# Low parts of attention values at byte 132 instead of 130, and two figures of the planner

## The chip, the cores and the metric

One NeuronCore of a Trainium2 chip runs the kernel. The metric is the device time of one launch in microseconds (us). Three runs of the kernel before took 1343.99, 1344.91 and 1344.94 us; their median is 1344.91.

The engines work side by side, each through its own list of instructions: TensorE (PE in the profile; PEld is its weight load), VectorE (DVE), ScalarE (ACT), GpSimd (POOL), and SyncE (SP), which here mainly issues DMA transfers. They wait for each other by semaphores.

## The reference

Two layers of a diffusion backbone over 1024 latent tokens and 256 context tokens of width 1024, in float32. Cut to what matters:

```python
for i in range(2):
    mod_x = (silu_c @ w_mod[i] + b_mod[i])[:, None, :]      # shift, scale and gate for the tokens
    mod_c = silu_cc @ w_mod[i] + b_mod[i]                   # the same for the context
    hx = rms_norm(x, norm_g[i]) * (1.0 + sc_x) + sh_x
    hc = rms_norm(ctx, norm_g[i]) * (1.0 + sc_c) + sh_c
    # layer A (i = 0): 16 query heads on 4 key/value heads, rotary positions, softmax over 1280 keys
    # layer B (i = 1): 16 heads, 8 x 16 neighbourhood on a 64 x 16 grid with a bias, plus 256 context keys
    #   o = softmax(q k^T / 8 [+ bias]) v ;  yx = (o * silu(z)) @ w_out
    x = x + g_x * yx
return rms_norm(x, final_norm_g)
```

The attention output is, for each query and head, a weighted sum of the value rows v (64 numbers per head). That sum is the place of the change.

## The kernel before

**Two halves for each number.** Matmul operands are float16. To keep float32 accuracy each operand is kept as a high part (the number rounded to float16) and a low part (the rest, rounded again), and a product is three matmuls: high x high, high x low, low x high.

**The value tiles.** Layer A keeps the values of all 1280 keys in `v1` (line 767): 128 partitions, 10 key blocks, 4 heads, and a row of 130 float16 numbers, 260 bytes. Numbers 0 to 63 of a row are the high part, 64 is a constant (so that the same matmul also sums the weights), and from 65 on comes the low part, 64 numbers from byte 130. One number is unused. Layer B has the same row in `v1_` (line 1490), for two heads at a time. ScalarE writes the high part and VectorE the low part by a subtraction (lines 891 and 892 in `kv_post`, lines 1546 and 1547 in `put_v`).

**Who reads them.** The softmax weights of a block of 128 queries are the stationary operand, the value row is the moving one, and the result is accumulated in PSUM.

- Layer A, `pv_mm` (lines 1136 to 1138), called by `a_att`: for each key block and each of four query blocks three matmuls, weights high x value high with the constant (65 columns), weights high x value low (64 columns, from byte 130), weights low x value high (65 columns).
- Layer A, `q_att` (lines 1211 and 1213), for a quarter of the heads' work, in which scores have the queries on the partitions and the weights are turned by a DMA transpose: one matmul with 128 columns, the high part and the low part as two runs of 64, and one of weights low x value high with 64 columns.
- Layer B, `b_att` (lines 1646, 1648, 1649): the same three as in `pv_mm`.

**Stages.** The start normalises the tokens and computes the modulation of layer A and its keys and values (0 to about 100 us). Then come eight head pairs of layer A, with the projections of the next pair mixed in (to about 700 us), layer A's output projection and the normalisation for layer B (to about 810 us), eight head pairs of layer B with projections mixed in (to about 1310 us), and the output projection with the last norm.

**Modulation matmuls.** They multiply float32 weights by two vectors only, so they use 32 of the 128 columns of the array each, four side by side. `quarters` (line 600) and `cols` (line 609, 2 columns of output) serve the start; `mod_block` (lines 633 and 637) computes the other shifts, scales and gates in 16 half blocks of 16 (every second one of 20) matmuls, spread over layer A's attention. The profile shows each of these float32 matmuls as two rows.

**What sets the order.** The program is first written in the order of the Python code, with a timeline that mixes the generators. Then the class `Planner` orders the instructions of each engine anew. `cost` gives each instruction a duration; `schedule` plays the program through with these, five engines side by side; `deadlines` works backwards from that to a due time for each instruction, in which TensorE's own start times count without their idle parts; `refine` repeats this five times and keeps the order whose planned end comes first; `apply` fixes it. The planner runs before the program is built, so its figures change the order of instructions and nothing else. For TensorE `cost` takes

```python
return max(cols * passes / 2.4 + 2.5, 29.0), 170.0
```

with `passes` 4 for float32, and `schedule` lets a matmul in a 32-column strip hold the engine for 7 ns if the strip differs from that of the matmul ahead (a quarter of its cost if it is the same).

Of the kernel before, what the change touches and what calls it, by code (L numbers as in the profile page):

```python
# [13 lines left out]
F16 = mybir.dt.float16  # L14
# [7 lines left out]
P = 128  # L22
# [6 lines left out]
HD = 64  # L29
# [13 lines left out]
class Planner:  # L43
# [72 lines left out]
    def cost(self, x, rd, wr):  # L116
# [6 lines left out]
        if e == "PE":  # L123
            f32 = ins[0].dtype == mybir.dt.float32
            cols = self.elems(outs[0])
            passes = (2 if x.is_transpose else 4) if f32 else 1
            if f32 and any("idf" in a.bass_ap.tensor.name for a in ins):
                passes = 2
            return max(cols * passes / 2.4 + 2.5, 29.0), 170.0
        if k == "InstDmaTransposeAnt":  # L130
# [159 lines left out]
    def schedule(self, key=None, margin=0.0, scale=None):  # L290
# [65 lines left out]
        while count < N:  # L356
# [43 lines left out]
            if e == "PE":  # L400
# [4 lines left out]
                if ts[1] < 128 and pe_last and pe_last[0] == ts and pe_last[1] != tp:  # L405
                    t[e] = max(s + 7, t[e])
                    pe_hold = max(pe_last[2], s + occ)
                    t[e] = s + 7
                    pe_last = (ts, tp, pe_hold)
                else:  # L410
                    if pe_last and pe_last[0] == ts and ts[1] < 128:
                        pass
                    t[e] = s + (occ if ts[1] == 128 else occ / 4)
                    pe_last = (ts, tp, s + occ)
# [41 lines left out]
    def deadlines(self, margin):  # L456
# [4 lines left out]
        for a in self.order["PE"]:  # L461
            idle += max(0.0, start[a] - prev)
            prev = max(prev, start[a] + (cst[a][0] if tuple(self.node[a].tile_size or (128, 128))[1] == 128
                                         else cst[a][0] / 4))
            due[a] = start[a] - idle
# [58 lines left out]
def trunk_kernel(ctx, tc, x, cx, cc, norm_g, ng_row, b_cols, sel_c, w_m0, w_mb, b_mod, a_wkv, a_wq, a_qg, a_kg, a_w_out,  # L524
# [241 lines left out]
    k2 = ap.tile([P, NKV, TOK], F16, name="k2")  # L766
    v1 = ap.tile([P, NT, NKV, 130], F16, name="v1")
    G.memset(k2[64:65], 1.0)
# [120 lines left out]
    def kv_post(ps, t):  # L889
        vv = ps[:, 256:512].rearrange("p (h d) -> p h d", d=HD)  # L890
        S.copy(v1[:, t, :, 0:HD], vv)
        V.tensor_tensor(v1[:, t, :, 65:129], vv, v1[:, t, :, 0:HD], op=ALU.subtract)
        k16 = norm_rope_split(lp, sqk, ps[:, 0:256].rearrange("p (h d) -> p h d", d=HD), None, 1, NKV, t, gck, gsk, gks,
# [238 lines left out]
    def pv_mm(pv, hi, lo, v, n, first, last):  # L1132

        for t in range(n):
            c = slice(t * P, (t + 1) * P)
            T.matmul(pv[:, t, :], hi[:, c], v[:, 0:65], start=first and t == 0, stop=False)  # L1136
            T.matmul(pv[:, t, 0:HD], hi[:, c], v[:, 65:129], start=False, stop=False)  # L1137
            T.matmul(pv[:, t, :], lo[:, c], v[:, 0:65], start=False, stop=last and t == n - 1)  # L1138
# [32 lines left out]
    def q_att(u, pt_):  # L1171
# [7 lines left out]
        for t in range(4):  # L1179
# [17 lines left out]
            for c, (k0, n) in enumerate(KCH):  # L1197
# [9 lines left out]
                def pvs(ppt=ppt, k=k, k0=k0, t=t):  # L1207
                    for x_ in range(k):
                        kt = k0 // P + x_
                        vv = v1[:, kt, g, :].rearrange("p (a b) -> p a b", b=65)[:, :, 0:HD]  # L1210
                        T.matmul(pv[:, t, :].rearrange("p (a b) -> p a b", b=HD), ppt[:, x_], vv,  # L1211
# [273 lines left out]
    def b_qk(u):  # L1485
# [3 lines left out]
        q2 = q2z[u % 2]  # L1489
        v1_ = bq.tile([P, NT, 2, 130], F16, name=f"bv1{u}", tag="v1")  # L1490
        G.memset(v1_[:, :, :, HD:HD + 1], 2.0 * WS * WS)
# [47 lines left out]
    def b_vz(u):  # L1539
# [3 lines left out]
        def put_v(src, ts):  # L1543
            n = len(range(NT)[ts])
            vv = src[:, 0:n * P].rearrange("p (t h d) -> p t h d", h=2, d=HD)
            S.copy(v1_[:, ts, :, 0:HD], vv)
            V.tensor_tensor(v1_[:, ts, :, 65:129], vv, v1_[:, ts, :, 0:HD], op=ALU.subtract)

# [37 lines left out]
    def b_att(u):  # L1586
# [14 lines left out]
        for hf in range(2):  # L1601
            og = bl.tile([P, 4, P], F32, name=f"bog{u}{hf}", tag="og", bufs=2)
            for i in range(2):
                tq = tabs[2 * u + i]
                pv = psum.tile([P, 4, P], F32, name=f"bpv{u}{i}{hf}", tag="pv", bufs=2)
                for t0 in (hf * 4, hf * 4 + 2):
# [21 lines left out]
                    for t in (t0, t0 + 1):  # L1628
# [15 lines left out]
                        def pvs(pv=pv, pht=pht, plt=plt, i=i, t=t, keys=list(near[t]) + [NX, NX + 1]):  # L1644
                            for x_, kt in enumerate(keys):
                                T.matmul(pv[:, t % 4, 0:65], pht[:, x_], v1_[:, kt, i, 0:65],
                                         start=t % 4 == 0 and x_ == 0, stop=False)
                                T.matmul(pv[:, t % 4, 0:HD], pht[:, x_], v1_[:, kt, i, 65:129], start=False, stop=False)
                                T.matmul(pv[:, t % 4, 0:65], plt[:, x_], v1_[:, kt, i, 0:65], start=False,
# [195 lines left out]
```

## Time and profile before

| | |
|---|---|
| runs | 1343.99, 1344.91, 1344.94 us |
| profiled execution | 1345.52 us, of which 1343.7 from the first to the last instruction |
| TensorE busy | 1309.6 us (97%) |
| VectorE, ScalarE, GpSimd busy | 1067.1, 969.0, 891.2 us |
| mean granted clock of TensorE | 0.992 of full speed |
| DMA | 191.64 MB, 143 GB/s on average |

Durations of matmuls overlap: a matmul starts while the ones before it are still on their way through the array. What one costs in a row of matmuls is the distance from its start to the next start, and the duration also holds its way through. "L1137" is line 1137 of the kernel. A row of a group gives the engine, the operation, output and inputs by their names in the program, the shape, the count, and busy time with the mean duration, or shortest, median and longest.

### The profile page before, as it was taken

What the parts mean: (1) busy time and instruction counts of PE and PEld (TensorE: products, weight loads), DVE (VectorE), ACT (ScalarE), POOL (GpSimd) and SP (SyncE); (2) the same over time, 40 slices, a digit from 0 to 9 for tenths busy, and PEclk for the clock granted to TensorE, in tenths of its full rate; (3) what the DMA queues carried; (4) which work ended last, traced back from release to release, by engine and by line L of the source; (5) the groups of instructions that cost most, each with busy time, mean ns of one, the idle gap of its engine ahead of it and who ended that gap; (6) DMA issues with size and microseconds to landing.
All of it is one profiled execution on the core that took longest, in us unless ns stands there. A gap on an engine that the chain in (4) does not pass through costs nothing.

```text
span 1343.7 us, 38645 instructions
## 1 busy us (share of the span) xinstructions
PE 1309.6 (97%) x15100; PEld 928.6 (69%) x15100; DVE 1067.1 (79%) x2456; ACT 969.0 (72%) x2076; POOL 891.2 (66%) x1214
## 2 busy tenths in 40 slices
PE   8999999999999999999999989999999999999996
PEld 4457777777777777776654457869687786968552
DVE  5898787888889787769528997878888888887665
ACT  4554889988888777798743456878878888887453
POOL 2323878777777767687876467677676868767543
PEclk9899999999999999999999999999999999999998
DMA  9633576786675222244317962678777877669952
GB/s 371 188 116 96 111 152 117 145 187 135 140 145 122 74 67 72 59 119 108 113 51 187 243 139 82 125 145 152 150 139 142 158 143 162 145 151 226 286 130 110
DMA packets 390496, 191.64 MB, mean 143 GB/s; under 512 B 349792, under 2 KB 355104, under 8 KB 390312
## 3 DMA queue, kind: packets, MB, share of 16 engines
q1 hardware_dynamic: 389736, 189.13, 62.1%
q8 instruction: 118, 1.93, 0.6%
q14 instruction: 66, 0.54, 0.1%
q10 hardware_dynamic: 576, 0.03, 0.0%
HBM read 91.03 MB, written 15.75 MB: 79 GB/s over the span
## 4 chain that ended last, share of the span: by engine, by line
PE 73%; DVE 10%; ACT 6%; DMA 5%; issue 3%; POOL 2%; DVEq 0%; POOLq 0%; SPq 0%; ACTq 0%
PE pa L1034 13%; PE poa L1358 6%; PE pob L1739 6%; PE st L1260 3%; PE st L1261 3%; PE pm L1068 3%; PE pkv L887 2%; PE pv L1137 2%; PE pv L1138 2%; PE pv L1136 2%; DMA bpht<-bph 2%; DMA qpp<-qpp 2%; PE pvc L1577 1%; PE qpv L1211 1%; PE pbc L1527 1%
## 5 line engine op out<-in xcount | busy, mean ns | idle before, releaser
L1130 POOL TENSOR_TENSOR pl<-pf,ph 128x256 f16<-128x256 f32 x400 | 274.9, 711 | 85.7 <-ACT pf L1247 56.2
L1130 POOL TENSOR_TENSOR bph<-bpf,bph 128x256 f16<-128x256 f32 (+1 forms) x224 | 184.0, 848 | 102.0 <-ACT bpf L1637 81.8
L1034 PE MATMUL pa<-wa,x 128*128 128x256 f16 x1536 | 219.8, 272 | 0.7 <-DVE q L822 0.7
L1245 ACT ACTIVATE ph<-st 128x512 f16<-128x512 f32 x240 | 143.8, 602 | 58.0 <-PE st L1261 56.2
L1565 PEld LDWEIGHTS <-hx 128*128 128x128 f16 x2688 | 157.3, 98 | 10.2 <-issue 1.3
L1034 PEld LDWEIGHTS <-x 128*128 128x128 f16 x1536 | 140.4, 97 | 33.3 <-issue 1.4
L1247 ACT ACTIVATE pf<-st 128x512 f32<-128x512 f32 x240 | 143.6, 604 | 2.0 <-DVE pl L1127 0.9
L1069 DVE TENSOR_REDUCE mxp<-pm 128x1 f32<-128x512 f32 x192 | 127.3, 683 | 12.8 <-PE pm L1068 11.7
L1137 PE MATMUL pv<-v,ph 128*128 128x64 f16 x960 | 122.4, 195 | 0.0
L1136 PE MATMUL pv<-v,ph 128*128 128x65 f16 x960 | 121.9, 193 | 0.2 <-ACT ph L1245 0.2
L1138 PE MATMUL pv<-v,pl 128*128 128x65 f16 x960 | 121.3, 192 | 0.0
L1130 POOL TENSOR_TENSOR qpp<-qpf,qpp 128x256 f16<-128x256 f32 (+1 forms) x158 | 93.4, 616 | 31.6 <-ACT qpf L1203 29.3
L1517 PEld LDWEIGHTS <-wb 128*128 128x128 f16 x672 | 63.9, 98 | 71.9 <-issue 6.6
L1635 ACT ACTIVATE bph<-bpf,bnx 128x384 f16<-128x384 f32 (+1 forms) x128 | 69.3, 581 | 52.4 <-DVE bnx L1627 33.8
L1136 PEld LDWEIGHTS <-ph 128*128 128x128 f16 x960 | 90.9, 97 | 22.1 <-ACT ph L1245 0.7
L1137 PEld LDWEIGHTS <-ph 128*128 128x128 f16 x960 | 90.4, 97 | 15.8 <-issue 0.4
L1138 PEld LDWEIGHTS <-pl 128*128 128x128 f16 x960 | 91.2, 99 | 9.3 <-POOL pl L1130 1.2
L1260 PE MATMUL st<-q,k 128*128 128x512 f16 x240 | 90.8, 379 | 0.7 <-ACT pf L1247 0.4
L1261 PE MATMUL st<-q,k 65*128 65x512 f16 x240 | 91.5, 381 | 0.0
L1358 PE MATMUL poa<-woa,oa 128*128 128x512 f16 x384 | 89.8, 379 | 0.0
L1739 PE MATMUL pob<-wob,obf 128*128 128x512 f16 x336 | 80.5, 379 | 1.9 <-DVE acc L1742 1.4
L1434 POOL TENSOR_TENSOR wtb<-wsb 128x256 f32<-128x256 f32 x64 | 56.5, 884 | 32.5 <-DMA wsb<-in_b_wp 17.0
(485 smaller groups left out, 4050.2 us busy)
## 6 DMA issues: line engine op xcount, KB each, us to landing
wg<-in_w_mb SPq DMA_DIRECT2D x32, 512.0 KB, 4.5
wsb<-in_b_wp SPq DMA_DIRECT2D x64, 256.0 KB, 2.8
wm<-in_w_m SPq DMA_DIRECT2D x16, 512.0 KB, 9.0
wsa<-in_a_wq SPq DMA_DIRECT2D x32, 256.0 KB, 3.5
xstage<-in_x SPq DMA_DIRECT2D x8, 512.0 KB, 5.6
wsoa<-in_a_w_out SPq DMA_DIRECT2D x16, 256.0 KB, 2.7
x<-in_x SPq DMA_DIRECT2D x8, 512.0 KB, 8.5
x_d<-x SPq DMA_DIRECT2D x8, 512.0 KB, 5.1
```

Source lines behind the costliest of these rows:

```text
L1034: T.matmul(ps[:, :, i, :], hA(a, kt, t), wt[w][:, kt, :], start=n == 0, stop=n == 3 * KT - 1)
L1130: G.tensor_tensor(lo[:, c], p32[:, c], hi[:, c], op=ALU.subtract)
L1136: T.matmul(pv[:, t, :], hi[:, c], v[:, 0:65], start=first and t == 0, stop=False)
L1137: T.matmul(pv[:, t, 0:HD], hi[:, c], v[:, 65:129], start=False, stop=False)
L1138: T.matmul(pv[:, t, :], lo[:, c], v[:, 0:65], start=False, stop=last and t == n - 1)
L1245: S.activation(ph, st, AF.Exp)
L1247: S.activation(p32, st, AF.Exp)
L1260: T.matmul(so, k1[:, g, kc], q1[:, :, i, :], start=True, stop=False)
L1261: T.matmul(so, k2[0:65, g, kc], q2[0:65, :, i, :], start=False, stop=True)
L1358: T.matmul(ps, lhs(a, kt), w[b][:, kt, :], start=n == 0, stop=n == 3 * KT - 1)
L1565: T.matmul(ps[:, t * P:(t + 1) * P], hx[a][:, t, blk, kt], wt[j][:, s_, w, kt], start=first and t == 0 and m == 0, stop=last and t == 3 an ...
L1739: T.matmul(ps, ob[kt][:, t, a], wout["b"][hf][b][:, kt, :], start=n == 0, stop=n == 3 * len(kts) - 1)
```

## The change

The row of a value tile gets 132 numbers (264 bytes) and its low part begins at number 66, byte 132, in both layers; all writers and readers follow. Number 65 is unused.

In the planner, three figures change. A matmul counts at least 30.4 ns instead of 29.0, and a float32 one with fewer than 8 output columns (line 609) at least 140. A matmul in a 32-column strip that differs from the strip of the matmul ahead holds the engine for 0.3 of its cost instead of 7 ns, and `deadlines` counts 0.3 of its cost instead of a quarter.

```diff
-            return max(cols * passes / 2.4 + 2.5, 29.0), 170.0
+            return max(cols * passes / 2.4 + 2.5, 140.0 if f32 and cols < 8 else 30.4), 170.0
...
-                    t[e] = s + 7
+                    t[e] = s + 0.3 * occ
...
-                                         else cst[a][0] / 4))
+                                         else cst[a][0] * 0.3))
...
-    v1 = ap.tile([P, NT, NKV, 130], F16, name="v1")
+    v1 = ap.tile([P, NT, NKV, 132], F16, name="v1")
...
-        V.tensor_tensor(v1[:, t, :, 65:129], vv, v1[:, t, :, 0:HD], op=ALU.subtract)
+        V.tensor_tensor(v1[:, t, :, 66:130], vv, v1[:, t, :, 0:HD], op=ALU.subtract)
...
-            T.matmul(pv[:, t, 0:HD], hi[:, c], v[:, 65:129], start=False, stop=False)
+            T.matmul(pv[:, t, 0:HD], hi[:, c], v[:, 66:130], start=False, stop=False)
...
-                        vv = v1[:, kt, g, :].rearrange("p (a b) -> p a b", b=65)[:, :, 0:HD]
+                        vv = v1[:, kt, g, :].rearrange("p (a b) -> p a b", b=66)[:, :, 0:HD]
...
-        v1_ = bq.tile([P, NT, 2, 130], F16, name=f"bv1{u}", tag="v1")
+        v1_ = bq.tile([P, NT, 2, 132], F16, name=f"bv1{u}", tag="v1")
...
-            V.tensor_tensor(v1_[:, ts, :, 65:129], vv, v1_[:, ts, :, 0:HD], op=ALU.subtract)
+            V.tensor_tensor(v1_[:, ts, :, 66:130], vv, v1_[:, ts, :, 0:HD], op=ALU.subtract)
...
-                                T.matmul(pv[:, t % 4, 0:HD], pht[:, x_], v1_[:, kt, i, 65:129], start=False, stop=False)
+                                T.matmul(pv[:, t % 4, 0:HD], pht[:, x_], v1_[:, kt, i, 66:130], start=False, stop=False)
```

## The prediction

> **What bounds the kernel now.** I read the page's totals and chain first, then the busy time by stage, then the matmul lines that the change touches, and last the starts of single matmuls.
>
> ```profile
> span 1343.7 us, 38645 instructions
> PE 1309.6 (97%) x15100; PEld 928.6 (69%) x15100; DVE 1067.1 (79%) x2456; ACT 969.0 (72%) x2076; POOL 891.2 (66%) x1214
> PE 73%; DVE 10%; ACT 6%; DMA 5%; issue 3%; POOL 2%; DVEq 0%; POOLq 0%; SPq 0%; ACTq 0%
> ```
>
> TensorE is busy for 97% of the span and holds 73% of the chain that ended last. The busy time by stage (stretch, length, then busy time and count of TensorE, its weight loads, VectorE, ScalarE, GpSimd; granted clock; DMA share) says where it binds:
>
> ```profile
> 0.00:96.00 96.00, 89.72 (x549) 46.44 (x550) 75.00 (x193) 50.24 (x102) 25.51 (x35) 0.95 0.67 228
> 144.00:432.00 288.00, 284.53 (x3659) 219.26 (x3656) 241.61 (x677) 250.19 (x580) 220.05 (x340) 1.00 0.71 141
> 432.00:624.00 192.00, 191.91 (x2580) 146.20 (x2578) 148.10 (x316) 150.19 (x305) 139.63 (x198) 1.00 0.29 74
> 816.00:1200.00 384.00, 380.44 (x5039) 294.37 (x5037) 324.36 (x734) 311.31 (x666) 283.78 (x383) 1.00 0.73 144
> 1306.00:1343.70 37.70, 26.51 (x124) 11.79 (x121) 21.08 (x37) 13.01 (x31) 12.61 (x13) 0.89 0.26 98
> ```
>
> From 432 to 624 us (attention of layer A, heads without the transposed path) TensorE idles 0.1 us in 192; from 816 to 1200 (layer B) 3.6 in 384; from 144 to 432 3.5 in 288, with ScalarE busy for 250. So nanoseconds taken from each attention matmul should come off the span nearly one for one in the second and third of these, less surely in the first. The start (6.3 us idle in 96) and the end (11.2 in 38) hold no attention matmul with low parts that matters.
>
> Now the value matmuls. Columns: engine, line, operation, out<-in, count, duration min/median/max in ns, first and last start in us.
>
> ```profile
> L1136 PE MATMUL pv<-v,ph x960: 190/193/205, 128.4 to 692.6; 128*128 128x65 f16 x192
> L1137 PE MATMUL pv<-v,ph x960: 191/195/205, 128.5 to 692.7; 128*128 128x64 f16 x192
> L1137 PE MATMUL pv<-v,phc x64: 193/195/198, 192.6 to 697.5; 128*128 128x64 f16 x64
> L1138 PE MATMUL pv<-v,pl x960: 190/192/204, 130.7 to 692.7; 128*128 128x65 f16 x192
> L1646 PE MATMUL bpv<-bv,bpht x608: 191/193/205, 839.3 to 1303.4; 128*128 128x65 f16 x152
> L1648 PE MATMUL bpv<-bv,bpht x608: 193/195/198, 839.3 to 1303.4; 128*128 128x64 f16 x152
> L1211 PE MATMUL qpv<-v,qpp x320: 217/221/232, 141.2 to 426.1; 128*128 128x128 f16 x160
> L1213 PE MATMUL qpv<-v,qpp x320: 189/193/193, 141.2 to 426.2; 128*128 128x64 f16 x160
> ```
>
> L1137 and L1648 are the matmuls with the low part, from byte 130. They have one column fewer than their neighbours and take 2 ns longer. What a matmul costs in a stream is the distance to the next start, so here are starts (us), durations, lines:
>
> ```profile
> 1076.35 0.20 PE L1648 MATMUL bpv<-bv,bpht 128*128 128x64 f16 x1
> 1076.39 0.19 PE L1649 MATMUL bpv<-bv,bpht 128*128 128x65 f16 x1
> 1076.41 0.19 PE L1646 MATMUL bpv<-bv,bpht 128*128 128x65 f16 x1
> 1076.44 0.20 PE L1648 MATMUL bpv<-bv,bpht 128*128 128x64 f16 x1
> 1076.48 0.19 PE L1649 MATMUL bpv<-bv,bpht 128*128 128x65 f16 x1
> 1076.51 0.19 PE L1646 MATMUL bpv<-bv,bpht 128*128 128x65 f16 x1
> ```
>
> After L1648 the next start is 0.04 us away, after the other two 0.02 to 0.03. Measured so over all rows of each line (those above give first, last and count; true waits of over 60 ns left out), the mean distance is 33.5 ns after L1137 and 33.6 after L1648; 29.2 to 29.8 after L1136, L1138, L1646 and L1649; 28.4 after L1213, which has 64 columns like L1137 but starts at the row's first byte; and 57.9 after L1211, half of whose 128 columns start at byte 130, against 56 for 128 columns in one piece (L1577, below). The Trainium skill, "TensorE: Matmul & The Clock Gate", section "Wait — 56ns, not 53.3ns?", gives columns over 2.4 GHz plus 2.5 ns, that is 29.2 ns for 64 columns and 29.6 for 65. The trace agrees with it for every value line except the two that start at byte 130.
>
> Rows of the value tile are 260 bytes apart, so every second high part starts at 4 but not 8 bytes of alignment, and L1136 shows no second group for it (median 193, 190 to 205). Four bytes seem to be enough, and 132 gives that to every low part.
>
> **The change part by part.**
>
> Low parts at 132. Taking each from its distance now to that of its 65-column neighbours in the same stream (29.2, the nearest row): 1024 x (33.5 - 29.2) = 4.4 us in layer A, 608 x (33.6 - 29.2) = 2.7 in layer B, and 320 x (57.9 - 56.0) = 0.6 at L1211. Sum 7.7 us. Upper bound by L1213's 28.4: 1632 x 5.2 + 0.6 = 9.1. Lower bound 0, if alignment is not the cause; a loss I exclude, since rows with the new alignment are already in the trace at 29. Where in layer A they lie:
>
> ```profile
> busy tenths in 40 slices 0000334333335667676750000000000000000000
> ```
>
> This is L1137 over the span. By its digits a good third comes before 432 us, together with all of L1211, where ScalarE is busy 250 of 288. There I let half of the gain go into later waits for ScalarE: (4.4/3 + 0.6)/2 = 1.0 us lost. Left: 6.7 us.
>
> VectorE's subtraction that writes the low part now writes at 4-byte alignment (columns: busy us, mean ns, then idle before):
>
> ```profile
> L892 DVE TENSOR_TENSOR v<-pkv,v 128x256 f16<-128x256 f32 x10 | 4.1, 417 | 0.1
> L822 DVE TENSOR_TENSOR q<-pa,q 128x256 f16<-128x256 f32 x40 | 16.6, 416 | 8.5 <-ACT q L821 8.5
> ```
>
> It takes 417 ns, the aligned subtraction of the same size 416: nothing to win or lose, with or without cover. Four bytes more per row move no other operand off its alignment.
>
> Planner figures. They change no instruction, only the order on each engine; every engine has the same set. Set side by side, the two orders differ by a median of 0 to 4 places, on TensorE at most 486 of 29000; the stages come in the same sequence, the modulation blocks within 6 us of their old place, and after the last value matmul 116 output matmuls are left instead of 131. Three things follow.
>
> 1. Value matmuls are planned 1 ns longer (30.4), against 29 to 33 in the trace. Nothing.
>
> 2. Modulation matmuls in 32-column strips: the plan counted 7 ns each, now 0.3 of the full cost, 0.3 x (128 x 4/2.4 + 2.5) = 65 ns for 128 columns. A half block has 16 of them, and the trace shows each as two rows:
>
> ```profile
> 318.78 1.08 PE L633 MATMUL pmg<-wg,s 128*32 128x128 f32 x32
>   DMA qpp<-qpp: 4.9, 10
>   DMA bpht<-bph: 8.3, 12
> ```
>
> One half block takes 1.08 us. The old plan has 16 x 7 = 0.11, the new 1.04, so TensorE used to fall 0.97 us behind its plan at each of 16 half blocks and now keeps to it. That lag gave everything TensorE needs later 0.97 us more than planned; without it, what is late next is what it waits for already: transposes by DMA (4.9 us in 10 waits at L1211, 8.3 in 12 at L1646, above), planned to land just in time. Bounds: above, 16 x 0.97 = 15.5 us if every lag had hidden a lateness of its size; below, the same row's waits at L1211 gone, -4.9 us, since a plan with true lengths can place them better. I take one wait of the size seen, 4.9/10 = 0.5 us, near the row that shows how late transposes came even with the lag.
>
> 3. The start. The third token tile is now loaded behind the first two modulation weights on SP's queue, and the second group of 8 modulation matmuls (16 rows) goes ahead of the first key/value matmuls:
>
> ```profile
> 14.19 1.39 PE L887 MATMUL pkv<-wkv,x 128*128 128x512 f16 x3 [1.45 <-ACT x L881]
> 16.15 1.08 PE L600 MATMUL pm<-wm,s 128*32 128x256 f32 x8
> ```
>
> If their weights have landed by 14.19 - 1.45 = 12.7 us they fill the 1.45 us in which TensorE now waits for ScalarE: a gain of up to 1.45 us. If they land only at 16.15, where they start now, L887 is held 1.96 us, and the conversions behind it. The loads stand at the same place in the queue, so both are possible; I take 0 and keep -1.5 to +2.
>
> Sum against the profiled execution, 1345.52 us with 1343.7 of span: 1345.5 - 6.7 + 0.5 = 1339.3. That execution is 0.6 us above the median of the runs (1344.91), so on the runs' scale that is 1338.7, and I forecast 1339 us, 0.4% less.
>
> **The rivals.**
>
> Weights, not alignment. L1136 and L1137 load the same columns of weights twice, and L1138 behind them another tile's. If the 4 ns belong to that third load, moving the values changes nothing.
>
> ```profile
> L1137 PEld LDWEIGHTS <-ph x960: 94/97/102, 128.4 to 692.6; 128*128 128x128 f16 x192
> L1138 PEld LDWEIGHTS <-pl x960: 94/99/103, 130.5 to 692.7; 128*128 128x128 f16 x192
> 1052.96 2.68 PE pvc L1577 x48
> ```
>
> For it: the load for L1138 takes 99 ns, not 97, and L1137 takes only 29 ns in the few places where another matmul stands between it and L1136. Against it: L1211, which shares no weights, also loses 2 ns, and a long matmul ahead could hide a slow read too. Time: 1344.9 + 0.5 = 1345.4 us. The Trainium skill, same page, section "Back-to-back issue gap", speaks for this rival: in a stream of load and matmul pairs both set the spacing, about 81 ns at 128 columns. The trace does not agree: 48 matmuls of 128 columns, each with its load, pass in 2.68 us, 56 ns each (the row of the chain above).
>
> The lost lag (ends slower). The mechanism of item 2 at its full size: at each of 16 half blocks what TensorE needs next has 0.97 us less, 0.4 of it covered by the plan's margins (100 and 300 ns), 0.57 x 16 = 9.1 us of new waits for transposes and exponentials between 140 and 640 us. 1344.9 - 6.7 + 9.1 = 1347.3 us. It outweighs the gain from 6.7/16 = 0.42 us a half block. For it: ScalarE has 38 us of slack in 288, so a lateness is made up slowly. Against it: from 432 to 624 all others have 40 us to spare in 192, and a wait met once is not met again at the next block unless the lateness has been built up anew.
>
> **How the numbers follow.** Forecast (the low parts run at their neighbours' pace and most of it arrives) 0.69; weights 0.17; lost lag 0.14. A measurement tells about 0.2%, 2.7 us, from no change. The forecast case ends faster by more in 0.65 and within it in 0.04. Weights: 0.03 faster, 0.08 same, 0.06 slower, as the new order falls. Lost lag: 0.02, 0.03, 0.09. Together 0.70, 0.15, 0.15. Range: low end 1344.9 - 9.1 - 1.5 (start) - 1 (waits gone by the new order) = 1333; high end 1347, which takes in the weights case with 1.6 us to spare and the lost lag up to nearly its full size.
>
> **What would show it.** Right: L1137 and L1648 at 193 ns or less and 29 ns to the next start, L1211 at 219; 432 to 624 us passing some 2 us sooner with TensorE as full. Wrong: 195 ns unchanged (weights); new idle of TensorE before L1211, L1136 or L1260 between 140 and 640 us, behind modulation blocks (lost lag); L887 starting after 16 us (the start). What would upset all of it is a new wait of several microseconds at a change of stage, 624 to 816 us, which the new order could bring and no row of the old trace prices.

## The result and the profile after

The changed kernel takes 1355.14 us in the median of five runs (1351.79 to 1357.51), the kernel before in the same rounds 1344.91 (1343.99 to 1346.47). The ratio is 1.0069 with a 95% interval of 1.0052 to 1.0086: 9.3 us slower by the ratio and 10.2 by the medians, where 6 us faster was forecast, and outside the range. The execution profiled took 1355.14 us, at a mean granted clock of 0.995, where the one before had 0.992; so the clock is not what made it longer.

First the totals of the page, for the changed kernel:

```profile
span 1353.4 us, 38618 instructions
PE 1310.4 (97%) x15100; PEld 925.4 (68%) x15100; DVE 1070.3 (79%) x2456; ACT 969.1 (72%) x2076; POOL 887.7 (66%) x1214
```

TensorE is busy for 0.8 us more than before (1310.4 against 1309.6) and idle for 43.0 us instead of 34.1 (span less busy). The span grew by 9.7, so 8.9 of it is new idle time. Its busy time was meant to shrink by 7.7 us and did not. The busy time by stage (columns as in the prediction):

```profile
0.00:96.00 96.00, 89.19 (x567) 46.61 (x568) 76.60 (x199) 52.23 (x105) 25.67 (x35) 0.98 0.69 233
144.00:432.00 288.00, 280.20 (x3587) 214.48 (x3585) 242.43 (x679) 246.68 (x572) 217.66 (x336) 1.00 0.73 140
432.00:624.00 192.00, 190.08 (x2537) 143.56 (x2536) 144.34 (x305) 148.07 (x299) 136.58 (x196) 1.00 0.31 71
816.00:1200.00 384.00, 379.28 (x5084) 295.33 (x5082) 326.45 (x727) 305.78 (x657) 282.69 (x386) 1.00 0.72 141
```

From 144 to 432 us TensorE idles 7.8 us, where it was 3.5; from 432 to 624, where it had idled 0.1, 1.9; from 816 to 1200 4.7 instead of 3.6; in the first 96 us 6.8 instead of 6.3. Two thirds of the new idle time lie in these two stretches of layer A's attention. In 432 to 624, where the others had 40 us to spare, 2537 matmuls pass instead of 2580. A stretch of fixed times holds other work in another order, so here is the same by landmarks: from the first L1137 to the last L1138, the attention of layer A, 578.1 us pass, where it was 569.1. These 9.0 us are nearly all of the 9.7; what the stages ahead of it and behind it gain and lose nearly cancels out.

The matmuls that read the low part, after:

```profile
L1137 PE MATMUL pv<-v,ph x960: 190/194/197, 127.0 to 700.2; 128*128 128x64 f16 x192
L1648 PE MATMUL bpv<-bv,bpht x608: 192/194/197, 847.6 to 1316.5; 128*128 128x64 f16 x152
L1211 PE MATMUL qpv<-v,qpp x320: 217/219/231, 140.8 to 425.6; 128*128 128x128 f16 x160
  DMA qpp<-qpp: 13.6, 14
  DMA bpht<-bph: 5.5, 12
```

The medians fell by 1, 1 and 2 ns, not to the neighbours' 192 or 193. The mean distance from a start to the next, measured as in the prediction over all rows of a line, is 32.8 ns after L1137 (33.4 in the kernel before), 33.1 after L1648 (33.6), and 57.0 after L1211 (57.9); 29.2 to 30.0 after L1136, L1138, L1646 and L1649, as before (L1646 alone falls, by 0.4). Most of the 4 ns is still there. (The prediction's 33.5 for L1137 becomes 33.4 when all waits above 60 ns are cut the same way in each kernel.) The last two rows are the idle time of TensorE and its weight loads before L1211 and before L1646, with its times: the wait for the transposes of layer A grew from 4.9 us in 10 to 13.6 in 14; that of layer B fell from 8.3 to 5.5. A load and its matmul often wait for the same transfer, and these rows then count the wait twice. TensorE's own idle time before L1211 (us, times, longest) is, before and after:

```profile
PE qpv L1211 <- DMA qpp<-qpp: 0.9, 2, 0.7
...
PE qpv L1211 <- DMA qpp<-qpp: 5.4, 6, 1.7
```

Two of the new waits, in the trace of the matmuls (in brackets the idle time before and its end):

```profile
115.42 0.59 PE L1068 MATMUL pm<-k,q 128*128 128x512 f16 x2 [1.92 <-issue]
...
200.22 0.23 PE L1211 MATMUL qpv<-v,qpp 128*128 128x128 f16 x1 [1.65 <-DMA qpp<-qpp]
```

The first stands before a query-key product at the beginning of layer A's attention, the second before a matmul on transposed weights. A measure that counts no wait twice is the gap: the distance from one float16 matmul's start to the next, less what the planner's formula `cols / 2.4 + 2.5` gives for the first one. Gaps of over 150 ns between 96 and 660 us sum to 19.6 us after and 10.6 before; those ahead of L1211 hold 6.9 (2.2 before), ahead of L1068 5.2 (1.9). About half (9.6 us) come 6 to 22 us behind a modulation block. The blocks are some 30 us apart, so gaps strewn by chance would do the same. Those ahead of L1211 do gather there: 5.4 of the 6.9 us lie within 12 us behind a block, where it was 0.5 of 2.2.

### The profile page after: what moved, and what is told of

The parts are those of the page before. It is cut to its first block, busy times and chain, and to the rows that moved or that the text cites. A ratio compares the mean times of both kernels' runs of the same rounds, so it can differ in the third digit from the quotient of the medians.

```text
span 1353.4 us, 38618 instructions
## 1 busy us (share of the span) xinstructions
PE 1310.4 (97%) x15100; PEld 925.4 (68%) x15100; DVE 1070.3 (79%) x2456; ACT 969.1 (72%) x2076; POOL 887.7 (66%) x1214
## 5 line engine op out<-in xcount | busy, mean ns | idle before, releaser
L1034 PE MATMUL pa<-wa,x 128*128 128x256 f16 x1536 | 223.9, 272 | 0.2 <-DVE q L822 0.2
L1034 PEld LDWEIGHTS <-x 128*128 128x128 f16 x1536 | 139.5, 98 | 33.8 <-issue 1.3
L1069 DVE TENSOR_REDUCE mxp<-pm 128x1 f32<-128x512 f32 x192 | 127.3, 684 | 14.3 <-PE pm L1068 13.9
L1137 PE MATMUL pv<-v,ph 128*128 128x64 f16 x960 | 122.1, 194 | 0.0
L1136 PE MATMUL pv<-v,ph 128*128 128x65 f16 x960 | 121.5, 193 | 0.0
L1138 PE MATMUL pv<-v,pl 128*128 128x65 f16 x960 | 120.8, 192 | 0.1
L1136 PEld LDWEIGHTS <-ph 128*128 128x128 f16 x960 | 90.7, 97 | 21.3 <-ACT ph L1245 0.4
L1137 PEld LDWEIGHTS <-ph 128*128 128x128 f16 x960 | 90.1, 97 | 15.3
L1138 PEld LDWEIGHTS <-pl 128*128 128x128 f16 x960 | 90.6, 98 | 8.9 <-POOL pl L1130 1.3
L1260 PE MATMUL st<-q,k 128*128 128x512 f16 x240 | 90.9, 379 | 1.1 <-ACT pf L1247 0.8
L1261 PE MATMUL st<-q,k 65*128 65x512 f16 x240 | 91.2, 381 | 0.0
L1358 PE MATMUL poa<-woa,oa 128*128 128x512 f16 x384 | 89.6, 379 | 0.0
```

The source lines that it names most:

```text
L1034: T.matmul(ps[:, :, i, :], hA(a, kt, t), wt[w][:, kt, :], start=n == 0, stop=n == 3 * KT - 1)
L1069: V.tensor_reduce(mxs[i][:, t, ch:ch + 1], pm, axis=AX.X, op=ALU.max)
L1137: T.matmul(pv[:, t, 0:HD], hi[:, c], v[:, 66:130], start=False, stop=False)
L1261: T.matmul(so, k2[0:65, g, kc], q2[0:65, :, i, :], start=False, stop=True)
```

## The experiments

All edits are on the kernel before unless an entry says the changed one. Times are medians; a difference in microseconds is the ratio less one, times the median of the kernel before in the same rounds. Where a row of 132 numbers is named, it is the data part of the change, whose diff stands above.

**1. The two parts alone.** The rows of 132 with the old planner's figures (the order on every engine is then that of the kernel before), and the three planner figures with rows of 130 (the order is that of the changed kernel).

> The kernel before with the low parts at byte 132 in rows of 264 bytes, and the planner's old figures: the order on every engine is exactly that of the kernel before. Theory (new order lost the time, padding gains little): the distance after the low-part matmuls (lines 1137 and 1648) falls by 0.5 ns only, as in the changed kernel (33.4 to 32.8, 33.6 to 33.1), 1632 x 0.5 + 320 x 0.9 = 1.1 us less: about 1343.5 us against 1344.9. Rival (the padding itself harms, or is undone by the order): slower than before, or 7 us faster as predicted.

> The kernel before with rows of 130 numbers and the planner's three new figures: the order on every engine is exactly that of the changed kernel. Theory: all of the loss is here, 1355 to 1357 us, waits of TensorE for DMA transposes before line 1211 near 13 us instead of 4.9. Rival (loss from the padding): near 1345 us.

Rows alone: 1343.76 us, ratio 0.9991 (0.9982 to 0.9999), 1.2 us less. Figures alone: 1354.6 us, ratio 1.0074 (1.0060 to 1.0088), 10.0 us more. The loss is wholly the order's, and the rows gain about a sixth of what was forecast. The value matmuls of the kernel with the rows alone:

```profile
L1137 PE MATMUL pv<-v,ph x960: 190/194/204, 127.1 to 690.5; 128*128 128x64 f16 x192
L1648 PE MATMUL bpv<-bv,bpht x608: 193/194/197, 837.9 to 1300.7; 128*128 128x64 f16 x152
```

They read as in the changed kernel: distances 32.8 and 33.1 ns. 1024 x 0.6 + 608 x 0.5 + 320 x 1.1 (L1211, 57.9 to 56.8) = 1.3 us, or 1.6 by the sums over the three matmuls (92.7 to 92.2 ns in layer A, 92.6 to 91.5 in layer B). The time shows 1.2.

**2. The planner's figures one by one.** First the two for strips, then the two for the floor:

```diff
-                    t[e] = s + 7
+                    t[e] = s + 0.3 * occ
...
-                                         else cst[a][0] / 4))
+                                         else cst[a][0] * 0.3))
```

> The kernel before with only the two figures for 32-column strips changed (0.3 of the cost in the schedule and in the due times); the floor of 29.0 stays. Lost-lag theory: this figure alone takes the lag away, so about 1354 us and waits before line 1211 of 10 us or more. Rival (any other order is worse by some microseconds, whichever figure changes it): somewhere between 1340 and 1360 with no tie to these waits.

> The kernel before with only the floor of 30.4 ns for a matmul and the 140 ns for two-column float32 matmuls; strips stay at 7 ns, so TensorE still falls about 1 us behind its plan at each of 16 half blocks. Lost-lag theory: within 3 us of before, 1342 to 1348 us, waits before line 1211 near 5 us. Rival (any other order is worse): 1350 us or more here too.

Strips alone: 1351.2 us, ratio 1.0049 (1.0036 to 1.0062), 6.6 us more. Floors alone (30.4 and 140): 1352.64, ratio 1.0057 (1.0042 to 1.0071), 7.7 more. Together they cost 10.0, not 14.3: the losses do not add. The floors, for which the prediction had "Nothing", lose as much as the strips. The idle row before L1211, loads included, has 10.6 us in 15 with the strips alone and 6.4 in 7 with the floors alone (4.9 in 10 before), so what is lost does not follow this wait. In the waits of TensorE (us, times, longest) the kernel with the floors alone has three that the kernel before lacks or has smaller:

```profile
PE qpv L1211 <- DMA qpp<-qpp: 2.7, 3, 1.2
PE pm L1068 <- DMA q<-q: 2.6, 2, 1.3
...
PE pmg L633 <- DVE q L822: 1.6, 1, 1.6
```

**3. Two smaller changes of the floor.** One counts only the float32 matmuls of few columns differently, 16 instructions of the first 48 us; the other raises the floor by 0.4 ns.

```diff
-            return max(cols * passes / 2.4 + 2.5, 29.0), 170.0
+            return max(cols * passes / 2.4 + 2.5, 140.0 if f32 and cols < 8 else 29.0), 170.0
...
-            return max(cols * passes / 2.4 + 2.5, 29.0), 170.0
+            return max(cols * passes / 2.4 + 2.5, 29.4), 170.0
```

> The kernel before with only the figure of 140 ns for the float32 matmuls of two output columns: 16 instructions of the first 40 us, nothing else of the planner. Theory (any new order loses against the one of before, whichever figure brings it): 1348 to 1355 us although the figure touches the start alone, with new waits far behind the start. Rival (lost lag, or the floor's 1 ns on each value matmul, are the causes): within 2 us of 1345.

> The kernel before with the planner's floor for a matmul at 29.4 ns instead of 29.0, which lengthens only matmuls of 64 columns and fewer, by 0.2 to 0.4 ns in the plan. Theory (any new order loses): 1348 to 1355 us. Rival (the floor of 30.4 costs because it is 1.4 ns off): within 2 us of 1345, as so small a figure can't matter by its size.

The 140 alone: 1350.4 us, ratio 1.0040 (1.0025 to 1.0055), 5.4 more. The idle row before L1211, in the kernel with the 140 alone:

```profile
  DMA qpp<-qpp: 10.6, 18
```

A figure for 16 instructions of the start has doubled the waits for transposes between 140 and 426 us, with every strip still counted at 7 ns. So new waits of this kind need no lost lag. The floor of 29.4: 1347.84, ratio 1.0017 (1.0008 to 1.0027), 2.3 more.

**4. Does any other order lose?** The floor moved the other way, and another figure, that of a DMA's landing, moved by 0.1 us to the safe side:

```diff
-            return max(cols * passes / 2.4 + 2.5, 29.0), 170.0
+            return max(cols * passes / 2.4 + 2.5, 28.6), 170.0
...
-                fin = dma + 1500
+                fin = dma + 1600
```

> Edit: the kernel before, the planner's floor of a matmul 28.6 instead of 29.0 ns; nothing else. Theory F (the order of before is a favourable one among those the planner can give, and any new plan loses): a figure moved as far in the other direction loses like 29.4 did, 2 to 5 us: 1347.5 us (1346.3 to 1350), with 10 us or more of waits behind the transposes before the 128-wide matmuls of layer A and before the query products, against 5 in the kernel before. Rival D (direction: larger figures are what does harm, since they move work later in the plan than it comes): a smaller figure loses nothing, 1344.0 us (1342.5 to 1345.5).

> Edit: the kernel before, a DMA's landing planned at 1600 instead of 1500 ns; nothing else. No figure of a matmul is changed, and the transposes are planned safer by 0.1 us each. Theory F: the new order loses 2 to 5 us though the figure is on the safe side: 1347.5 us (1346.3 to 1350). Rival D: no loss, since at 2500 there was none: 1344.5 us (1343 to 1345.8).

The floor of 28.6: 1348.13 us, ratio 1.0019 (1.0007 to 1.0031), 2.6 more, as the floor of 29.4. A landing at 1600 ns: 1352.11, ratio 1.0057 (1.0037 to 1.0077), 7.7 more. Neither the direction nor the size of the figure tells what is lost here; what all have in common is another order. The waits that I had expected with these losses did not come: L1211 waits 2.0 us in 5 with the floor of 28.6 and 6.6 in 10 with 1600. The executions profiled took 1345.09 us and 1347.94, though, near the low end of their runs (1343.88 to 1351.29 and 1347.94 to 1357.21), so these traces do not show where the loss lies.

**5. What the waits for transposes are worth.** A DMA's landing planned at 2500 ns instead of 1500, in the changed kernel and in the one with the rows alone; and in the changed kernel the due times 600 ns ahead instead of 300.

```diff
-                fin = dma + 1500
+                fin = dma + 2500
```

> The changed kernel with one more figure of the planner: a DMA lands 2500 ns after its transfer instead of 1500. Theory (new orders lose where transposes are planned just in time): waits before line 1211 fall from 13.6 us to under 5, and the time from 1355 to under 1349. Rival (the order of before is merely one of the good draws, and no figure of this kind brings it back): 1348 to 1360 us, with the waits elsewhere.

> The kernel before with low parts at byte 132 and only the landing of DMAs planned at 2500 ns; the other figures are the old ones. Theory: transposes with more room, at or below the 1343.8 us of the padding alone. Rival (any new order loses): 1347 to 1354 us.

> The changed kernel with due times 600 ns ahead instead of 300. Theory (work that TensorE waits for is planned too late): waits before line 1211 halve, 1345 to 1350 us. Rival (orders lose as drawn): 1348 to 1360 us whatever the margin.

The changed kernel with 2500: 1348.68 us, ratio to the kernel before 1.0025 (1.0012 to 1.0037); 6 us of the changed kernel's loss are gone, 3.4 remain. The kernel with the rows alone and 2500: 1343.87, ratio 0.9985 (0.9975 to 0.9994), level with the rows alone (0.9991). Due times at 600: 1355.4, ratio 1.0066 (1.0044 to 1.0089); nothing gained. The idle rows before L1211 and L1646, with the rows alone and landings at 1500:

```profile
  DMA qpp<-qpp: 4.1, 8
  DMA bpht<-bph: 6.6, 10
```

The same with landings at 2500:

```profile
  DMA qpp<-qpp: 0.2, 1
  DMA bpht<-bph: 0.5, 2
```

The waits of TensorE and its loads for transposes are gone, 10.7 us down to 0.7; of TensorE's own 3.9 us among them (1.2 at L1211, 2.7 at L1646) none is left. Yet the time stays, and TensorE's idle time over the span too (34.1 and 33.8 us): gaps of over 150 ns between 96 and 660 us sum to 11.6 us where they were 10.5, now at L1068, L1260 and L1186. In the changed kernel with 2500 the row before L1211 still has 10.2 us in 7, though under 5 was expected; the time below 1349 came without that.

**6. Is a late landing the cure, or was 2500 a good draw?** With the rows of experiment 9, landings at 2500, 2600 and 3500 ns:

> Edit: as the kernel with the low part first, and a DMA's landing planned 2500 ns after it instead of 1500; the order on every engine is that of the kernel with 132 bytes and 2500. Theory S: 1.4 us below that one's 1343.9, so 1342.5 us (1341.0 to 1344.0), with no wait at the 128-wide matmuls of layer A on their transposes. Rival: 1343.9 (1342.9 to 1344.9), the same as with 132 bytes.

> Edit: as the kernel with the low part first, a DMA's landing planned at 2600 ns. With 2500 the same kernel took 1343.1 us. Theory L (planning the landings late is what keeps a new order from losing, since the matmuls then stand behind transposes that have come): 1343.1 us (1342 to 1344.5), and the waits for the transposes at the 128-wide matmuls below 1.5 us in the rows of PE and its loads together. Rival R (2500 was one more draw among orders, a good one): another 0.1 us draws again, 1346 us or more (1345 to 1350).

> Edit: as the kernel with the low part first, a DMA's landing planned at 3500 ns. Theory L: the waits for transposes stay below 1.5 us, and the time at 1343.1 (1342 to 1345), later only as far as work is put off needlessly. Rival R: 1346 us or more (1345 to 1352), with the waits at other places.

At 2500: 1343.11 us, ratio 0.9982 (0.9972 to 0.9992); at 2600 1345.01, ratio 0.9994 (0.9984 to 1.0005); at 3500 1349.9, ratio 1.0040 (1.0025 to 1.0055). The same rows with the old order have 0.9985 (experiment 9). The 1343.11 at 2500 lies in the ranges of both its theory and its rival, so it does not tell them apart. Against the old order 2600 costs some 1.2 us, which is within the intervals, and 3500 some 7.4, which is not. The kernel with 3500 waits for transposes for 2.0 us in 2, loads included; its other waits stand elsewhere:

```profile
PE pwv0c L1565 <- ACT wb L1438: 3.1, 1, 3.1
PE st L1260 <- ACT pf L1247: 1.5, 5, 0.5
...
PE pr L1108 <- DVE zmax L1084: 1.3, 1, 1.3
...
PE qpv L1211 <- DMA qpp<-qpp: 0.8, 1, 0.8
```

A late landing takes most of the waits for transposes away, as the first theory said (at 3500 not quite below its 1.5 us), and the time does not follow them, as the second did. The order at 2500 is a good one, and of its two neighbours one loses little or nothing and one much.

**7. Weights or address?** The three value matmuls in another order, so that low weights x high values comes second and the low part third:

```diff
-            T.matmul(pv[:, t, 0:HD], hi[:, c], v[:, 65:129], start=False, stop=False)
-            T.matmul(pv[:, t, :], lo[:, c], v[:, 0:65], start=False, stop=last and t == n - 1)
+            T.matmul(pv[:, t, :], lo[:, c], v[:, 0:65], start=False, stop=False)
+            T.matmul(pv[:, t, 0:HD], hi[:, c], v[:, 65:129], start=False, stop=last and t == n - 1)
```

> The kernel before with the last two of the three value matmuls exchanged in both layers (weights high x value high, weights low x value high, weights high x value low), so that no weights are loaded twice in a row; the planner orders the program anew. Theory W: no value line has more than 30 ns to the next start, 7 us of TensorE time less. Theory A or the low part itself: 33 ns stays with the low-part matmul, now the third. The time holds a new order too, which is worth 6 to 10 us either way by the runs so far: 1338 to 1352 us under W, 1345 to 1355 otherwise.

In this kernel L1649 holds the low part. Starts in a stream of layer B:

```profile
1077.87 0.19 PE L1646 MATMUL bpv<-bv,bpht 128*128 128x65 f16 x1
1077.90 0.20 PE L1648 MATMUL bpv<-bv,bpht 128*128 128x65 f16 x1
1077.93 0.19 PE L1649 MATMUL bpv<-bv,bpht 128*128 128x64 f16 x1
1077.96 0.19 PE L1646 MATMUL bpv<-bv,bpht 128*128 128x65 f16 x1
1077.99 0.19 PE L1648 MATMUL bpv<-bv,bpht 128*128 128x65 f16 x1
1078.02 0.19 PE L1649 MATMUL bpv<-bv,bpht 128*128 128x64 f16 x1
1078.06 0.19 PE L1646 MATMUL bpv<-bv,bpht 128*128 128x65 f16 x1
```

The long distance has gone with the low part: over all rows 33.5 ns after L1138 and 33.4 after L1649, 29.5 after L1137 (now low weights), 30.1 after L1648. The load of the other tile's weights is not its cause. The time is 1349.27 us, ratio 1.0030 (1.0016 to 1.0043), 4.0 more, again under another order.

**8. The start address by itself.** Two benches at the start of the kernel, behind the warming matmuls: twenty triples in each group, 65, 64 and 65 columns, each with its weight load, accumulated into a tile that nobody reads. The group with the low part at byte 130 and other weights is

```python
for n in range(20):
    T.matmul(A, W[0], ones[:, 0:65], start=False, stop=False)
    T.matmul(B, W[2], ones[:, 65:129], start=False, stop=False)
    T.matmul(A, W[1], ones[:, 0:65], start=False, stop=False)
```

> The kernel before with seven groups of 20 triples of matmuls put behind the warming matmuls at the start (about 13 us more; their sums are thrown away). Each triple has 65, 64 and 65 columns. Groups: (1) second matmul from byte 130, with the weights of the first loaded again, as in the kernel; (2) the same from byte 132; (3) byte 130 with other weights than its neighbours; (4) byte 132 with other weights; (5) byte 0 with the first one's weights; (6) three times 65 columns from byte 0 with three weights; (7) like (1) but into another part of the PSUM bank. Theory W (loading the same weights twice in a row delays the load after it): the distance from the second start to the third is 33 ns in 1, 2, 5 and 7, and 29 in 3, 4, 6. Theory A (any start that is not at the row's first bytes): 33 in 1 to 4 and 7, 29 in 5 and 6. Theory R (the third adds to the columns of the second too soon): 33 wherever the second has 64 columns, 29 in 7.

> As the first bench: ten groups of 20 triples (65, 64, 65 columns, three different weights) at the start. First and third read from number f of their row, the second from number s: (f, s) = (0,1), (0,2), (0,4), (0,8), (0,16), (0,32), (0,64), (0,128), (64,0), (66,0); byte offsets are twice that. The first bench gave 91.5 ns a triple with s = 65, 90.8 with 66 and 89.5 with 0. If the boundary that counts is 4 bytes, groups with s = 2 and more take 89.5; if it is 8, 16, 32 or 64 bytes, the sum drops from s = 4, 8, 16 or 32 on; if any start away from that of the neighbours costs, all groups take 91.

Rows of the first bench for the second matmul of a triple: byte 130 and the first's weights, byte 132 and the first's weights, byte 0.

```profile
L846 PE MATMUL idle<-ones x20: 194/194/196, 10.7 to 12.4; 128*128 128x64 f16 x20
...
L850 PE MATMUL idle<-ones x20: 193/194/194, 12.5 to 14.2; 128*128 128x64 f16 x20
...
L862 PE MATMUL idle<-ones x20: 190/191/193, 19.3 to 21.0; 128*128 128x64 f16 x20
```

Mean distances from all starts of each group (waits left out), after the second matmul and for the whole triple:

| second matmul starts at byte | weights of the second | after it, ns | triple, ns |
|---|---|---|---|
| 130 | the first's | 33.4 | 91.8 |
| 132 | the first's | 32.8 | 91.1 |
| 130 | others | 33.4 | 91.8 |
| 132 | others | 32.8 | 91.1 |
| 130, other part of PSUM | the first's | 33.4 | 91.8 |
| 0 | the first's | 28.5 | 90.0 |
| 0, and 65 columns like the other two | others | 30.2 | 90.8 |
| 2 | others | 30.4 | 91.0 |
| 4 | others | 30.6 | 89.3 |
| 8 | others | 30.9 | 89.3 |
| 16 | others | 28.7 | 89.6 |
| 32 | others | 28.4 | 90.0 |
| 64 (first 17 triples) | others | 28.8 | 89.8 |
| 256 | others | 28.4 | 89.8 |
| 0, the other two at 128 | others | 28.6 | 90.0 |
| 0, the other two at 132 | others | 28.4 | 90.0 |

(The expectations name 91.5, 90.8 and 89.5 ns for the triples at 130, 132 and 0; all starts of these groups give 91.8, 91.1 and 90.0.) Neither the weights nor the place in PSUM matter, the start bytes of the three do. No boundary of 4, 8 or more bytes explains the table: bytes 4 and 132 are aligned alike, and the triples take 89.3 and 91.1. And a triple whose second matmul takes 28.4 ns gives most of it back at the first, which then takes 28 to 30 ns or 35 to 37: byte 0 saves 4.9 ns after the second matmul and 1.8 over the triple. Some of the cost has no odd start at all: in the group of three times 65 columns from byte 0, a distance of 35 ns follows every fifth matmul, whichever of the three it is, and the others are 29 and 30. So the gap to the neighbours was the wrong measure: the least that any group reached is 89.3 ns a triple, 2.5 below byte 130, while the prediction took 4.3. With 1632 triples that is 4.1 us at the most, and byte 132 has 0.7 x 1632 = 1.1 of it. The group with the second matmul at byte 128 can't be read, and that at byte 64 only in its first 17 triples: there the clock went down, as the stretch of the second bench's trace shows that holds the end of the one and the other (last columns: granted clock, DMA share, GB/s),

```profile
24.00:28.00 4.00, 4.00 (x91) 4.00 (x87) 2.86 (x6) 3.26 (x8) 1.10 (x2) 0.59 1.04 401
```

and so does the long mean duration of the second matmul at byte 128 (count, busy us, mean ns of one, idle before):

```profile
L870 PE MATMUL idle<-ones 128*128 128x64 f16 x20 | 3.2, 239 | 0.0
```

**9. The better row.** The low part at the start of its row and the high part with its constant at byte 128, rows of 260 bytes and order as before:

```diff
-            T.matmul(pv[:, t, :], hi[:, c], v[:, 0:65], start=first and t == 0, stop=False)
-            T.matmul(pv[:, t, 0:HD], hi[:, c], v[:, 65:129], start=False, stop=False)
-            T.matmul(pv[:, t, :], lo[:, c], v[:, 0:65], start=False, stop=last and t == n - 1)
+            T.matmul(pv[:, t, :], hi[:, c], v[:, 64:129], start=first and t == 0, stop=False)
+            T.matmul(pv[:, t, 0:HD], hi[:, c], v[:, 0:64], start=False, stop=False)
+            T.matmul(pv[:, t, :], lo[:, c], v[:, 64:129], start=False, stop=last and t == n - 1)
```

> Edit: the kernel before, with the low part of the values at number 0 of its row and the high part with the 65th number at 64 to 128 (so byte 128), rows of 130 as before; the planner's figures are those of before and the order on every engine is that of before. Theory S (the start byte of the moving operand sets the 4 ns, and only a part of it comes back): in the second bench the sum of a triple with (65 numbers from 64, 64 numbers from 0) was 90.0 ns, against 91.5 for (0, 65) and 90.8 for (0, 66) in the first; 1.5 ns less for 1568 triples is 2.4 us: the distance after the low-part matmul 28.5 to 29.5 ns, that after the first 31 to 32.5, and 1342.5 us (1341.3 to 1343.7), 1.4 us below the kernel with 132 bytes alone. Rival (benches do not carry over, since the kernel loads fresh weights): the distances stay 33 to 34 ns at the second matmul and the time at 1344.9 (1344.0 to 1346.0).

1343.15 us, ratio 0.9985 (0.9977 to 0.9994), 2.0 us less than before. Against the rows of 132 (0.9991) it is lower too, but there the intervals overlap. Its rows:

```profile
L1137 PE MATMUL pv<-v,ph x960: 190/192/204, 127.8 to 690.3; 128*128 128x64 f16 x192
...
L1138 PE MATMUL pv<-v,pl x960: 191/194/204, 130.0 to 690.4; 128*128 128x65 f16 x192
```

L1137 has come down to 192, and L1138 has taken the 194: distances 30.2, 28.8 and 32.3 in layer A, 29.9, 29.5 and 32.2 in layer B. The cost was expected after the first matmul and stands after the third. A triple takes 91.2 and 91.6 ns, where it took 92.7 and 92.6; with L1211 (57.9 to 56.4) and L1213 (28.4 to 28.9, since it reads from byte 128 now) that is 1.5 x 1024 + 1.0 x 608 + 1.5 x 320 - 0.5 x 320 = 2.5 us. The bench's difference for these rows, 1.8 ns a triple, carries over in the main; the 4 ns do not come back in any row tried.

## Why the prediction was wrong

The forecast had 6.7 us less for the rows and 0.5 more for the order; measured apart, these are 1.2 less and 10.0 more. So the term for the order is off by 9.5 us and that for the rows by 5.5.

**What bounds it** was right: TensorE, 97% busy. What the two new rows take off its distances (1.3 to 1.6 us with 132 bytes, 2.5 with the low part first) arrives in the time nearly whole (1.2 and 2.0).

**Low parts at 132** (-7.7 us, -6.7 after the waits): wrong in size. The place was right, since the start byte does set the distance, and the rival "weights" falls by its own test (experiment 7), though its time for the rows, no change, was by luck the nearer one. The step that failed reads the 4.3 ns as what 4-byte alignment would give back, "Four bytes seem to be enough". In its place: 0.6 ns a matmul, 1.3 us in all, measured as 1.2. Two readings led there. The neighbours, which start at the row's first byte, differ from the low part in more than 4-byte alignment, and the distance after one matmul of a triple isn't what the triple can save. The sentence "a loss I exclude" held.

The columns-over-2.4-GHz-plus-2.5 rule of the Trainium skill ("TensorE: Matmul & The Clock Gate", section "Wait — 56ns, not 53.3ns?") gives 88.3 ns for a triple of 65, 64 and 65. No group measured comes below 89.3, and the kernel's triples take 91.2 to 92.8, so the measurement decides: for these triples the rule is 1.0 to 4.5 ns too short. Part of that hangs on the operands' start bytes and part does not (90.8 with all three at byte 0 and 65 columns, where the rule gives 88.8). For a single distance the rule is no floor either: 28.4 ns follow L1213's 64 columns, where it gives 29.2.

**VectorE's subtraction, 0**: nothing in the runs speaks against it; the kernel with the rows alone is faster, not slower.

**Planner, item 1, "Nothing"**: wrong by the largest single amount. The floors alone lose 7.7 us. The step took a figure near the trace for a harmless one, but what a figure does is choose an order, and how near it is to the trace did not matter: 28.6 and 29.4 lose alike, 2.6 and 2.3 us.

**Item 2, strips (+0.5, bounds -4.9 to +15.5)**: the size was within the bounds (6.6 alone) and the value taken far too low. The lateness did show where it was said to, at the transposes before L1211, with 13.6 us for 4.9 (5.4 for 0.9 of TensorE's own). But the mechanism of the rival "lost lag" isn't shown. It should have needed the strips, and with the strips at 7 ns the 140 and the landing of 1600 lost 5.4 and 7.7 us. It isn't excluded as a part of what the strips cost: within 12 us behind a block lie 5.4, 6.3 and 4.1 us of the gaps ahead of L1211 in the changed kernel, with the figures alone and with the strips alone, and 0.5 to 2.2 before and in the five kernels with one other figure (floors, 140, 29.4, 28.6, 1600). That rival's time, 1347.3, was too low as well.

**Item 3, the start (0, bounds -1.5 to +2)**: held. The modulation matmuls did go ahead, before their weights had landed:

```profile
14.08 0.88 PE L600 MATMUL pm<-wm,s 128*32 128x256 f32 x8 [0.91 <-DMA wm<-in_w_m]
15.27 1.08 PE L600 MATMUL pm<-wm,s 128*32 128x256 f32 x8 [0.31 <-DMA wm<-in_w_m]
16.28 1.03 PE L887 MATMUL pkv<-wkv,x 128*128 128x512 f16 x2
```

L887 starts at 16.28 us, the sign that the prediction named for a loss. It was made up: the first L1137 starts at 127.0 us, and at 127.1 with the rows alone and the old order.

**What was left out** decides it. The step that failed is "Three things follow": the prediction priced a new order by three effects that it could name and put all else at nothing. The runs show in its place that the order of before is a favourable one, and that most figures that lead to another order lose. Twelve plans that differ from that of before, with the time against the old order with the same rows:

| figures changed | rows | us |
|---|---|---|
| strips, floors (the changed kernel's three) | 130 | +10.0 |
| strips | 130 | +6.6 |
| floors 30.4 and 140 | 130 | +7.7 |
| 140 | 130 | +5.4 |
| floor 29.4 | 130 | +2.3 |
| floor 28.6 | 130 | +2.6 |
| landing 1600 | 130 | +7.7 |
| the three, landing 2500 | 132 | +4.6 |
| the three, due times 600 | 132 | +10.1 |
| landing 2500 | 132 | -0.8 |
| landing 2600 | low part first | +1.2 |
| landing 3500 | low part first | +7.4 |

The landing of 2500 lost nothing, with the low part first neither (-0.4), and that of 2600 can't be told from nothing; the other ten lost. This is shown as a fact of the runs. Why those orders lose is settled only in part. In the changed kernel the new time is mostly idle time of TensorE in layer A's attention, in waits for transposes, query copies and exponentials, and when one kind is planned away others take its place. With the floor of 29.4 not even that holds: its execution profiled is 4.3 us longer than that of before, and 2.7 of it is busy time of TensorE (1312.3 us). What property of the order decides it is open. So is in part why executions of one order can differ by 9 us among themselves (landing 1600); the granted clock goes with it there, as the three shorter ones (1347.94 to 1350.62 us) had 0.995 to 0.997 and the three longer ones (1353.59 to 1357.21) 0.993 to 0.994. The chance of 0.15 for slower was too low for a change that replans 15,000 matmuls.

## What to carry to other kernels

Where a planner or scheduler fixes the order, test a change of its figures and a change of the data apart, and judge a figure against a few neighbours of it: here a shift of 0.4 ns or of 0.1 us cost 2.3 to 7.7 us, where the data part gained 1.2. Price a stream by the sum over its repeating group, not by the gap that one member has to its neighbours, since what is taken from one matmul may come back at the next. And taking away the wait that the profile names is no gain by itself: TensorE's waits for transposes went, 3.9 us of its own idle time, other waits came, and the time stayed. Before such a wait is priced, see whether a matmul and its load count it twice.

## What the runs showed of the hardware

- The distance between matmuls of 64 and 65 float16 columns depends on where the moving operands start: with the neighbours at byte 0 a triple takes 91.0 ns with the middle one at byte 2, 89.3 at 4 and at 8, 89.6 at 16, 90.0 at 32, 91.8 at 130, 91.1 at 132 and 90.0 at 0. From byte 2 to 4 it falls by 1.7 ns and from 130 to 132 by 0.7, and what sets the rest wasn't found.
- The cost moves within the triple: at byte 130 after the second matmul (33.4, the others 29), at byte 0 after the first (mean 32.0), and in the kernel with the low part first after the third (32.3).
- Repeated weights and another place in PSUM changed nothing (33.4 in each case).
